# One core, a mixture-of-experts block and a second block: expert biases loaded ahead, the latents' path without GpSimd, late modulation chunks placed anew, the rotary low part in full height

## The chip, the cores and the metric

One Trainium2 chip, one of its cores. The metric is the device time of one execution in microseconds (us), the median of several runs. Besides TensorE (PE), VectorE (DVE), ScalarE (ACT) and GpSimd (POOL) the core has SyncE (SP), which here does nothing but issue loads.

## What is computed

Two transformer blocks on 256 tokens of width 1024, all in 32 bits. The change lies in the first, between its projections and its experts:

```python
m = silu(c) @ w_mod + b_mod                      # 6 chunks of 1024: sh1 sc1 g1 sh2 sc2 g2
hx, hc = modulate(x, g, sh1, sc1), modulate(ctx, g, csh1, csc1)
px, pc = hx @ w_in, hc @ w_in                    # fourier 256, q latent 384, kv latent 256, rope 64
q  = rms_norm(q_lat, norm_q) @ w_q_up            # 6 heads of 128 + 64 rotary
kv = rms_norm(kv_lat, norm_kv) @ w_kv_up         # 6 heads of 128 + 128
att = softmax(q @ k.T * 192**-0.5) @ v           # k from x and from ctx: 512 keys
x  = x + g1 * rms_norm(concat(att, fourier(px)) @ w_out, norm_attn_post)
h  = modulate(x, norm_ffn_pre, sh2, sc2)
logits = h @ w_router + b_router; top 4 of 32 experts for each token
g = min(xb @ w_gate[e] + b_gate[e], 7); u = clip(xb @ w_up[e] + b_up[e], -7, 7)
y = (g * sigmoid(1.702 * g) * (u + 1)) @ w_down[e] + b_down[e]
x  = x + g2 * rms_norm(sum of gates * y, norm_ffn_post)
```

A second block follows (two mixers, two MLPs), which the change does not touch.

## The kernel before, in words

**The stream.** All large weights come in pieces of up to 1 MB through one list of jobs (class `Stream`). Each job has a ring of tiles of its own: ring A (7 tiles), B (6), and C (3), D (2) and E (3), which are opened in SBUF that earlier stages give back. SP issues the loads strictly in the order of the list (line 161); each waits until its tile's earlier content has been read, and a load that waits holds up all behind it. The loads use eight completion semaphores in turn, and a load waits as well until the load that had its semaphore before has landed, whichever engine issued that one. `also` adds small loads behind a job. Ring E is opened by `open_ring` at the start of `moe`, when the tiles of `pre_finish` are free. The expert part of the list is, for each expert, four pieces of `w_gate`, four of `w_up` and four of `w_down`; 21 tiles in all can be ahead.

**Exact products.** Most matmuls before the experts run on pairs: a weight piece is split into a rounded part (ACT) and the rest (a subtraction on DVE, in some cases on POOL: `QA`, `split_aside`), and `mm3` makes three matmuls of them. `prepare` does the splits ahead; ring B holds the pairs.

**The late modulation.** `pre_project` computes sh1 and sc1. The other four chunks of `m` come as 16 pieces of 1 MB, eight for columns 2048 to 4095 (n = 1) and eight for 4096 to 6143 (n = 2). `modulation` takes the next piece: one of n = 1 is four matmuls into the bank `macc` (lines 317 to 319); one of n = 2 is multiplied by `silu(c)` and added into `msum` in four pieces of 512 columns, two of which go to DVE (`scalar_tensor_tensor`, line 311) and two to ACT (line 313) and POOL (line 314). `mod_sum` sums `msum` over the partitions on TensorE, and `mod_fin` turns a result row into columns (ACT copies it to `mrow`, line 329; TensorE transposes it, line 332). The order is all of n = 2, then all of n = 1, and the tables `QMOD`, `MODS` and `FILLS` say how many pieces are taken at which place.

**Latents to attention.** At the end of `pre_project` the latents are scaled by their gains and split, and ACT squares them; POOL adds the squares over the groups of 128 (line 577). `latent_scales` sums them over partitions (`ms`, line 592), takes the root and the reciprocal, and spreads the row over all partitions (diagonals `dgl` on DVE, line 600; `bc`, line 604). It is a generator, called piece by piece from `q_up`, which makes the queries: three weight pairs of 27 matmuls each. `pre_attend` then makes the keys `kn` of six heads, the rotary parts, the values `vt`, and the attention in six steps u (three pairs of heads, two query blocks). A step is `begin(u)` (scores, line 747), `turn(u - 1)` (transposes, line 779), `scores(u)` (the rotary part: `krh` at line 754 with all 128 rows, its low part `krl` at line 755 with the 64 rows of one head; then the softmax on DVE and ACT, lines 759 to 770), and `values` (line 790), with the pieces of `FILLS` at the end. `out_part` is the output projection, whose last matmuls run beside the start of `pre_finish`.

**Into the experts.** `pre_finish` puts small jobs between the parts of the output projection: `bias_rows`, `expert_bias_in` and `bias_split` among them. `expert_bias_in` (line 953) loads the gate and up biases of all experts by four loads on ACT's queue (line 957) and the down biases by four more (line 960); `bias_split` (lines 968 and 971) splits them on ACT and DVE. Only then come, on ACT and DVE, `gained` (lines 888 and 890), `added` (line 899), `turned` (line 905), the norm, the router's logits (line 916), `choose` and the ranks, and the experts' first gather and matmul (lines 1291 and 1208).

## Time and profile before

| what | value |
| --- | --- |
| median of 3 runs | 1835.69 us (1834.64 to 1837.01) |
| the profiled execution's own time | 1836.42 us |
| its span, first to last instruction | 1834.6 us |
| TensorE busy | 1732.3 us, 94% |
| VectorE busy | 752.9 us, 41% |
| ScalarE busy | 589.9 us, 32% |
| GpSimd busy | 57.9 us, 3% |
| bytes moved | 553.45 MB, mean 302 GB/s |

Times in the trace count from the start of the span. A row of the trace names the source line, the engine, the operation, what it writes and reads by the program's names, and how often; several equal instructions in a row are merged into one. What stands in brackets is the idle time of the engine before it and what ended that. TensorE's matmuls on 32 bits appear as two instructions each.

### The profile page before, as it was taken

What the parts mean: (1) busy time and instruction counts of PE and PEld (TensorE: products, weight loads), DVE (VectorE), ACT (ScalarE), POOL (GpSimd) and SP (SyncE); (2) the same over time, 40 slices, a digit from 0 to 9 for tenths busy, and PEclk for the clock granted to TensorE, in tenths of its full rate; (3) what the DMA queues carried; (4) which work ended last, traced back from release to release, by engine and by line L of the source; (5) the groups of instructions that cost most, each with busy time, mean ns of one, the idle gap of its engine ahead of it and who ended that gap; (6) DMA issues with size and microseconds to landing.
All of it is one profiled execution on the core that took longest, in us unless ns stands there. A gap on an engine that the chain in (4) does not pass through costs nothing. (4 is left out here: it accounts for less than half of the span.)

```text
span 1834.6 us, 24464 instructions
## 1 busy us (share of the span) xinstructions
PE 1732.3 (94%) x9537; PEld 1038.8 (57%) x9537; DVE 752.9 (41%) x1582; ACT 589.9 (32%) x1158; POOL 57.9 (3%) x52
## 2 busy tenths in 40 slices
PE   7889599999999989999989988899999999999998
PEld 6756553333333323333323332388689989989997
DVE  4786242222222212222211211476675558756555
ACT  4544221111111101111111110355654445555444
POOL 0340000000000000000000000100000001000000
PEclk9989799999999999999999999999999999999999
DMA  9767599999999999999999999987245554435540
GB/s 350 262 242 265 197 356 405 412 412 411 410 412 413 412 412 412 410 411 412 412 413 412 413 411 411 338 249 230 70 161 186 185 188 154 132 116 203 185 158 23
DMA packets 202525, 553.45 MB, mean 302 GB/s; under 512 B 11136, under 2 KB 87558, under 8 KB 200358
## 3 DMA queue, kind: packets, MB, share of 16 engines
q1 hardware_dynamic: 201026, 549.82, 79.4%
q8 instruction: 76, 1.25, 0.3%
q10 hardware_dynamic: 932, 1.29, 0.2%
q0 software_dynamic: 448, 0.73, 0.1%
q14 instruction: 43, 0.35, 0.1%
HBM read 550.71 MB, written 1.07 MB: 301 GB/s over the span
## 5 line engine op out<-in xcount | busy, mean ns | idle before, releaser
L1565 DVE TENSOR_TENSOR ring<-ring,ring 128x1024 fp32r<-128x1024 f32 x196 | 230.6, 1221 | 78.2 <-ACT ring L1564 77.6
L1208 PE MATMUL g<-ring,xg 128*64 128x512 f32 x1056 | 254.0, 603 | 8.1 <-DMA ring<-in_w_gate 8.1
L1208 PE MATMUL u<-ring,xg 128*64 128x512 f32 x1056 | 248.2, 602 | 10.7 <-DMA ring<-in_w_up 9.7
L1219 PE MATMUL y<-ring,ht 128*64 128x512 f32 x1056 | 241.1, 599 | 15.9 <-DMA ring<-in_w_down 15.4
L1564 ACT CAST ring<-ring 128x1024 fp32r<-128x1024 f32 x196 | 195.3, 1049 | 75.7 <-PE acc L1794 54.3
L1280 ACT ACTIVATE z<-y,gsl 64x512 fp32r<-64x512 f32 x66 | 45.0, 682 | 428.6 <-PE y L1219 401.6
L1779 PE MATMUL ot<-ahi,ring 128*128 128x256 f32 x960 | 177.2, 282 | 0.0
L1219 PEld LDWEIGHTS y<-ring,ht 128*64 128x64 f32 x1056 | 69.9, 136 | 164.6 <-issue 117.6
L1281 DVE SCALAR_TENSOR_TENSOR z<-y,gsl,z 64x512 fp32r<-64x512 f32 x66 | 49.5, 750 | 250.6 <-ACT z L1280 250.5
L1779 PEld LDWEIGHTS ot<-ahi,ring 128*128 128x128 f32 x960 | 151.3, 191 | 1.3
L1208 PEld LDWEIGHTS u<-ring,xg 128*64 128x64 f32 x1056 | 67.3, 136 | 132.5 <-issue 98.9
L1208 PEld LDWEIGHTS g<-ring,xg 128*64 128x64 f32 x1056 | 66.9, 136 | 126.9 <-issue 118.7
L1779 PE MATMUL ot<-alo,ring 128*128 128x256 f32 x480 | 135.6, 283 | 0.0
L1794 PE MATMUL acc<-ring,hhi 128*128 128x512 f32 x480 | 131.5, 395 | 0.0
L1794 PEld LDWEIGHTS acc<-ring,hhi 128*128 128x128 f32 x480 | 88.1, 188 | 19.0
L1227 ACT ACTIVATE sg<-gm 128x512 f32<-128x512 f32 x33 | 20.8, 630 | 238.8 <-DVE gm L1226 238.8
L1779 PEld LDWEIGHTS ot<-alo,ring 128*128 128x128 f32 x480 | 91.8, 191 | 1.3
L1293 ACT ACTIVATE xg<-xg,mod,a 128x128 f32<-128x128 f32 (+1 forms) x136 | 50.9, 452 | 98.3 <-PE xg L1291 98.3
L1779 PE MATMUL pj<-ahi,ring 128*128 128x256 f32 x416 | 80.0, 287 | 0.0
L1291 PEld LDWEIGHTS xg<-pm,x 128*128 128x128 f32 x544 | 63.7, 191 | 26.2 <-issue 14.6
L1270 DVE TENSOR_SCALAR gt<-gt,cp 128x256 fp32r<-128x256 f32 x33 | 16.0, 484 | 150.4 <-PE gt L1268 150.4
L1794 PE MATMUL acc<-ring,hlo 128*128 128x512 f32 x240 | 75.4, 395 | 0.0
(520 smaller groups left out, 2157.2 us busy)
## 6 DMA issues: line engine op xcount, KB each, us to landing
ring<-in_w_gate SPq DMA_DIRECT2D x128, 1024.0 KB, 18.1
ring<-in_w_up SPq DMA_DIRECT2D x128, 1024.0 KB, 18.1
ring<-in_w_down SPq DMA_DIRECT2D x128, 1024.0 KB, 18.1
ring<-in_mlp_w SPq DMA_DIRECT2D x64, 1024.0 KB, 5.3
ring<-in_w_mod SPq DMA_DIRECT2D x24, 1024.0 KB, 7.0
ring<-in_odd_w_in SPq DMA_DIRECT2D x12, 1024.0 KB, 5.7
ring<-in_even_w_in SPq DMA_DIRECT2D x7, 1024.0 KB
ring<-in_w_out SPq DMA_DIRECT2D x4, 1024.0 KB, 5.4
```

The costliest lines, as they stand in the source:

```text
L1208: nc.tensor.matmul(acc[64 * h : 64 * h + 64], xg[:, 2 * q + j], w[:, j, 512 * h : 512 * h + 512], start=(q == 0 and j == 0), stop=False, s ...
L1219: nc.tensor.matmul(acc[64 * h : 64 * h + 64], l, w[:, j, 512 * h : 512 * h + 512], start=(q == 0 and j == 0), stop=(q == 3 and j == 1), sk ...
L1227: nc.scalar.activation(sg, gm, AF.Sigmoid, scale=1.702)
L1270: nc.vector.tensor_scalar(gt, b, self.c("misc")[:, 0:1], None, OP.is_equal)
L1280: nc.scalar.mul(t[s], a[s], g[s])
L1281: nc.vector.scalar_tensor_tensor(t[o], a[s], g[s], t[s].bitcast(F32), OP.mult, OP.subtract)
L1291: nc.tensor.matmul(b[:, n * j : n * j + n], self.x[:, t, (k + j) * P : (k + j + 1) * P], pm[:, t, 0:n], start=(t == 0), stop=(t == 1))
L1293: nc.scalar.activation(xg[:, k + j], b[:, n * j : n * j + n], AF.Identity, bias=self.mod[:, 0, 24 + k + j : 25 + k + j], scale=self.a2[:, ...
L1564: nc.scalar.copy(hi[:, c], v[:, c])
L1565: nc.vector.tensor_tensor(lo[:, c], v[:, c], hi[:, c].bitcast(F32), OP.subtract)
L1779: nc.tensor.matmul(out, w[a][:, k, c : c + n], x[b][:, k], start=(k == 0 and i == 0), stop=(k == KD - 1 and i == 2))
L1794: nc.tensor.matmul(acc[2 * t + n], x[a][kx][:, t * P : (t + 1) * P], w[b][:, j, 512 * n : 512 * n + 512], start=(first and i == 0), stop=( ...
```

## The change

- `expert_bias_in` now only lists the four loads of the gate and up biases, into tiles of their own, and the stream issues them on SP behind the first piece of `w_out`. The four loads of the down biases go to POOL's queue (`down_bias_in`).
- POOL has no arithmetic left before the experts: all subtractions of the splits of `w_q_up` and `w_kv_up` are on DVE, the squares are summed over the groups by TensorE in `latent_scale`, and all four parts of an n = 2 piece are on DVE (the first piece on ACT).
- `latent_scale` is called for the query latent after the first weight pair and for the kv latent after the second, each followed by its `spread`. The split at the end of `pre_project` falls away; the copy of `krp` goes from DVE to ACT.
- The 16 late pieces come in the order `LATE`: one after each weight pair of `q_up`, one after each head's keys, one in each quarter of the values, and one in each of the attention's first three steps. `mod_sum` follows its last piece directly.
- The rotary low part has two tiles of 128 rows, one for each head of a pair, the other head's rows set to zero.

```diff
-MODS, FILLS = (0, 1, 0, 1, 0, 1, 2, 1, 1, 2), (1, 2, 1, 2, 0)
-QMOD, KVA, SMALL, QA, EARLY = 1, 3, 0, 2, 3
+LATE = (1, 1, 1, 2, 1, 2, 1, 2, 1, 2, 2, 2, 2, 1, 1, 2)
+QMODS, MODS, FILLS = (1, 1, 1), (1, 1, 1, 1, 1, 1, 1, 1, 1, 1), (1, 1, 1, 0, 0)
+SMALL, EARLY = 0, 3
...
-                for g in (0, 2, 1, 3):
+                for g in range(4):
                     o, v = self.msum[:, 512 * g : 512 * g + 512], w[:, 512 * g : 512 * g + 512]
                     if k == 0:
                         nc.scalar.mul(o, v, c)
-                    elif g > 1:
+                    else:
                         nc.vector.scalar_tensor_tensor(o, v, c, o, OP.mult, OP.add)
-                    else:
-                        nc.scalar.mul(v, v, c)
-                        nc.gpsimd.tensor_tensor(o, o, v, OP.add)
+                if k == KD - 1:
+                    self.mod_sum()
...
-                (nc.gpsimd if aside else nc.vector).tensor_tensor(l[:, :, i], vv[:, :, i, c0:c1], h[:, :, i].bitcast(F32), OP.subtract)
+                nc.vector.tensor_tensor(l[:, :, i], vv[:, :, i, c0:c1], h[:, :, i].bitcast(F32), OP.subtract)
...
+                ("o", 3): self.expert_bias_in(B)}
...
-        self.late = [(n, k) for n in (2, 1) for k in range(KD)]
+        late = self.late = [(n, LATE[:i].count(n)) for i, n in enumerate(LATE)]
...
-        nc.vector.tensor_copy(krp, br)
+        nc.scalar.copy(krp, br)
-        for s, n in ((sq, 3), (sk, 2)):
-            for j in range(1, n):
-                nc.gpsimd.tensor_tensor(s[:, 0], s[:, 0], s[:, j], OP.add)
-        st.prepare()
...
+    def latent_scale(self, C, i):
+        s, t0, n = self.sq[i], 2 * i, 2 + 2 * i
+        m = s.shape[1]
+        bs = self.bank("ms", "s")
+        for t in range(n):
+            for j in range(m):
+                nc.tensor.matmul(bs[:, 2 * t : 2 * t + 2], s[:, j, t * P : (t + 1) * P], self.c("ones")[:, 0:2], start=(j == 0), stop=(j == m - 1))
+        r = self.r6[:, 2 * t0 : 2 * (t0 + n)]
+        nc.scalar.activation(r, bs[:, 0 : 2 * n], AF.Sqrt, bias=self.eps[1e-6], scale=1.0 / (128 * m))
+        nc.vector.reciprocal(r, r)
+        dg = C.tile([P, 4, P], F32, tag="prob", name="dgl", bufs=3)
+        for t in range(n):
+            nc.vector.tensor_scalar(dg[:, t], self.c("ident"), r[:, 2 * t : 2 * t + 1], None, OP.mult)
+        def spread():
+            b = self.bank("bc", "s")
+            nc.tensor.matmul(b[:, 0 : n * P], self.c("ones"), dg[:, 0:n].rearrange("p a b -> p (a b)"), start=True, stop=True)
+            nc.scalar.copy(self.rqk[:, t0 * P : (t0 + n) * P], b[:, 0 : n * P])
+        return spread
...
-            next(scales, None)
+            if q < 2:
+                spread = self.latent_scale(C, q)
...
-            if q == QMOD:
-                self.modulation()
+            self.modulation(QMODS[q])
+            if q < 2:
+                spread()
...
+        kr[2] = B.tile([P, 512], F32R, tag="krp", name="krl1")
+        zero = self.c("tri")[:, 0:1].to_broadcast([P, 512])
+        nc.scalar.copy(kr[2][0:64], zero[0:64])
+        nc.scalar.copy(kr[2][64:P], kr[1][64:P].bitcast(F32))
+        nc.vector.tensor_copy(kr[1][64:P], zero[64:P])
...
-                nc.tensor.matmul(b, l[o], kr[1][o], start=False, stop=True)
+                nc.tensor.matmul(b, l, kr[1 + i], start=False, stop=True)
...
-        fills = {u: [self.mod_sum] * (u == 2) + [self.modulation] * FILLS[u] + [gains] * (u == 4) for u in range(5)}
+        fills = {u: [self.modulation] * FILLS[u] + [gains] * (u == 4) for u in range(5)}
...
-        fills = [lambda: self.bcast_row(C, self.gc, g1b, bank="b"), router, lambda: self.bias_rows(B), lambda: self.expert_bias_in(B, R),
+        fills = [lambda: self.bcast_row(C, self.gc, g1b, bank="b"), router, lambda: self.bias_rows(B), lambda: self.down_bias_in(R),
...
-            t = self.braw[nm] = B.tile([P, 512], F32, tag=tag, name="braw")
+            t = self.braw[nm] = B.tile([P, 512], F32, name=f"{nm}r")
             for h in range(2):
-                self.nc.scalar.dma_start(out=t[64 * h : 64 * h + 64], in_=bass.AP(tensor=b.tensor, offset=b.offset + 512 * h, ap=[[0, 2], [D, E], [1, 512]]))
+                loads.append((t[64 * h : 64 * h + 64], bass.AP(tensor=b.tensor, offset=b.offset + 512 * h, ap=[[0, 2], [D, E], [1, 512]])))
...
-            self.nc.scalar.dma_start(out=self.bdn[E * q : E * q + E], in_=self.I["b_down"][0][:, T * q : T * q + T])
+            self.nc.gpsimd.dma_start(out=self.bdn[E * q : E * q + E], in_=self.I["b_down"][0][:, T * q : T * q + T])
```

Three places show how the order of instructions moves. The first is ACT's queue at the end of the output projection (`braw` are the raw biases, `bdn` those of the down matrices, `bkt` a small row for the second block). Before:

```order
L262 COPY gu<-bc 128x512 x2
L1695 ACTIVATE bkt<-bk 16x384
L957 DMA braw<-in_b_gate 64x1x512 x2
L957 DMA braw<-in_b_up 64x1x512 x2
L960 DMA bdn<-in_b_down 32x256 x4
L968 CAST b_gate<-braw 128x512
L968 CAST b_up<-braw 128x512
L888 ACTIVATE jk,s_1678<-mix 128x512 x2
```

and of the change:

```order
L265 COPY gu<-bc 128x512 x2
L1696 ACTIVATE bkt<-bk 16x384
L969 CAST b_gate<-b_gater 128x512
L969 CAST b_up<-b_upr 128x512
L885 ACTIVATE jk,s_1673<-mix 128x512 x2
```

The loads have left this queue, and the two casts read the tiles that the stream loads. The four loads now stand in SP's queue, behind the first of the four `w_out` pieces:

```order
L164 DMA ring_1036<-in_w_mod 128x2048
L164 DMA ring_1066<-in_w_out 128x2x1024
L164 DMA b_gater<-in_b_gate 64x1x512 x2
L164 DMA b_upr<-in_b_up 64x1x512 x2
L164 DMA ring_1092<-in_w_out 128x2x1024
L164 DMA ring_1114<-in_w_out 128x2x1024
```

Three `w_out` pieces and all the experts' pieces are queued behind them. The third place is DVE from the rotary keys to the attention's first softmax. Before:

```order
L718 TENSOR_TENSOR krl<-krp,krh 128x512
L311 SCALAR_TENSOR_TENSOR msum<-ring_825,csil,msum 128x512 x2
L311 SCALAR_TENSOR_TENSOR msum<-ring_827,csil,msum 128x512 x2
L311 SCALAR_TENSOR_TENSOR msum<-ring_829,csil,msum 128x512 x2
L311 SCALAR_TENSOR_TENSOR msum<-ring_831,csil,msum 128x512 x2
L1677 COPY vc_1119<-bk 128x64
```

and of the change:

```order
L711 TENSOR_TENSOR krl_1039<-krp,krh 128x512
L716 CAST krl_1039<-cp 64x512
L314 SCALAR_TENSOR_TENSOR msum<-ring_886,csil,msum 128x512 x4
L314 SCALAR_TENSOR_TENSOR msum<-ring_930,csil,msum 128x512 x4
L314 SCALAR_TENSOR_TENSOR msum<-ring_944,csil,msum 128x512 x4
L314 SCALAR_TENSOR_TENSOR msum<-ring_976,csil,msum 128x512 x4
L1678 COPY vc_1138<-bk 128x64
```

DVE has 16 accumulations here where it had 8; the 8 additions that POOL made beside them are gone.

## Rows read from the trace of the kernel before

**Rows 1.** Busy by stretch (start:end us; length, busy us per engine, granted clock, DMA share, GB/s).
```profile
1000.00:1100.00 100.00, 90.30 (x418) 32.89 (x418) 18.75 (x38) 13.32 (x28) 0.00 (x0) 1.00 1.03 411
```

**Rows 2.** Queue of SP, who waited for whom: us in total, times, longest us.
```profile
SPq L161 <- DMA braw<-in_b_gate: 17.6, 1, 17.6
...
SPq L161 <- DMA braw<-in_b_up: 15.3, 2, 7.9
```

**Rows 3.** SyncE's queue in order of time around 229 us (start us, us, what).
```profile
229.00 0.88 SPq L161 DMA_DIRECT2D ring<-in_w_down  x2
```

**Rows 4.** ScalarE in order of time, 191 to 214 us (in brackets: idle before, releaser).
```profile
191.26 1.24 ACTq L957 DMA_DIRECT2D braw<-in_b_gate  x2
...
213.46 0.62 ACT L968 CAST b_up<-braw 128x512 fp32r<-128x512 f32 x1 [12.58 <-DMA braw<-in_b_up]
```

**Rows 5.** TensorE in order of time, 191 to 238 us.
```profile
191.09 8.46 PE L361 MATMUL mix<-ring,mix 128*128 128x512 f32 x36
...
218.32 1.94 PE L905 MATMUL bk<-cp,x 128*128 128x128 f32 x8 [18.77 <-DVE x L899]
...
220.08 3.62 PE L916 MATMUL lb<-wr,x1T 128*128 128x32 f32 x16
...
236.14 1.94 PE L1208 MATMUL g<-ring,xg 128*64 128x512 f32 x8
```

**Rows 6.** VectorE in order of time, its last operation on the biases.
```profile
214.11 1.38 DVE L971 TENSOR_TENSOR b_up<-braw,b_up 32x512 fp32r<-32x512 f32 x2 [11.81 <-ACT b_up L968]
```

**Rows 7.** Busy by stretch as in rows 1, the stretch of the routing.
```profile
215.00:229.00 14.00, 10.68 (x50) 10.26 (x50) 7.89 (x21) 8.38 (x20) 0.00 (x0) 0.50 0.55 222
```

**Rows 8.** TensorE in order of time: four forms at full clock.
```profile
120.50 1.07 PE L319 MATMUL macc<-ring,csil 128*32 128x512 f32 x8
...
139.34 0.48 PE L754 MATMUL sc<-krh,qs 128*128 128x512 f32 x1
...
139.74 0.49 PE L755 MATMUL sc<-krl,qs 64*128 64x512 f32 x1
...
157.41 1.04 PE L779 MATMUL tr<-cp,prob 128*128 128x128 f32 x8
```

**Rows 9.** TensorE in order of time, the query projection, 70 to 78 us.
```profile
70.03 0.50 PE L592 MATMUL ms<-cp,sqk 128*128 128x2 f32 x4
...
77.08 1.19 PE L604 MATMUL bc<-dgl,cp 128*128 128x256 f32 x2 [3.21 <-DVE dgl L600]
```

**Rows 10.** VectorE by line and form, 60 to 125 us: count, busy us, mean ns.
```profile
L311 DVE SCALAR_TENSOR_TENSOR msum<-ring,csil,msum 128x512 f32<-128x512 f32 x14 | 21.7, 1605 | 0.0
...
L566 DVE SCALAR_TENSOR_TENSOR lk<-bk,vc,lk 128x512 fp32r<-128x512 f32 x2 | 1.4, 748 | 1.6 <-ACT lk L565 1.6
```

**Rows 11.** VectorE in order of time, first step of the attention.
```profile
124.98 1.27 DVE L759 TENSOR_REDUCE mx<-sc 128x1 f32<-128x512 f32 x2
```

**Rows 12.** TensorE in order of time, steps of the attention.
```profile
127.90 1.97 PE L779 MATMUL tr<-cp,prob 128*128 128x128 f32 x8 [2.33 <-DVE prob L770]
...
155.69 1.88 PE L747 MATMUL sc<-kn,qn 128*128 128x512 f32 x4
...
161.73 1.88 PE L747 MATMUL sc<-kn,qn 128*128 128x512 f32 x4
```

**Rows 13.** DMA queues from 190 to 216 us: packets, MB, share of 16 engines.
```profile
q10 hardware_dynamic: 456, 0.66, 8.2%
```

**Rows 14.** ScalarE in order of time, the second split of the output projection.
```profile
162.38 2.01 ACT L1564 CAST ring<-ring 128x1024 fp32r<-128x1024 f32 x2
```

**Rows 15.** Busy by stretch as in rows 1, four stretches before the experts.
```profile
120.00:146.00 26.00, 21.14 (x86) 9.12 (x85) 15.66 (x35) 7.69 (x18) 3.72 (x3) 0.80 0.81 311
...
146.00:166.00 20.00, 19.24 (x89) 10.83 (x85) 12.54 (x29) 8.10 (x17) 0.00 (x0) 1.00 0.60 211
...
166.00:196.00 30.00, 29.77 (x138) 23.48 (x139) 11.70 (x27) 9.93 (x17) 0.56 (x1) 1.00 0.74 287
...
196.00:229.00 33.00, 14.23 (x66) 12.88 (x64) 10.14 (x24) 10.54 (x24) 0.00 (x0) 0.60 0.59 207
```

More of the change, by code (lines that the diff above doesn't have):

```diff
@@ L614, in q_up @@
         held = []
[L615 to L616 removed]
+        self.r6 = C.tile([P, 12], F32, name="r6")
+        self.rqk = B.tile([P, 768], F32, name="rqk")
         for q in range(3):
@@ L629, in q_up @@
                 held = []
-            if q == 1:
-                next(scales)
             st.prepare()
-            if q == QMOD:
-                self.modulation()
+            self.modulation(QMODS[q])
+            if q < 2:
+                spread()
+        self.msum = B.tile([P, 2048], F32, tag="sqk", name="msum")
     def pre_attend(self, B, C):
```

48 lines of the change are left out of this document (12 added, 36 removed).

## The prediction

> **What bounds the kernel now.** I read the page first, then busy time by stretch, then the waits of SP's queue, and last the time lines of the engines from 60 to 240 us. The long middle, the experts, is bound by loading: late in it the DMA engines are full at 411 GB/s, while TensorE has work for 90 of 100 us [rows 1]. The experts' last weight therefore lands a fixed time after the moment from which the loads run without a break. That moment is when ring E opens and the last three of the 21 tiles can be filled, at 229.00 us [rows 3], 7 us before the experts' first matmul at 236.14 [rows 5]. What comes after the experts waits for them. So the change is worth what it moves this moment, and I follow the path to it.
>
> Two places on that path are to be seen. The large one: TensorE ends the output projection at 191.09 + 8.46 = 199.55 us and then waits 18.77 us for `added` on DVE [rows 5]. ACT issued the bias loads at 191.26, and its cast of the up biases ran only at 213.46, after an idle time put down to that load [rows 4]; DVE's subtraction follows at 214.11 [rows 6], and everything of `pre_finish` is queued behind these on both engines. The same loads held up SP's queue for 17.6 and 15.3 us [rows 2]. The granted clock of the stretch behind the idle time is 0.50, the lower of the two levels, 1.2 GHz [rows 7]. The second: the attention's first reduction runs at 124.98 [rows 11], behind DVE's accumulations of the late modulation, which took 1605 ns in the mean, where the same operation at the same size takes 748 when POOL does nothing [rows 10].
>
> **The change, part by part.** *The bias wait.* From the end of DVE's last bias operation, 214.11 + 1.38 = 215.49, to the transposes at 218.32 [rows 5, 6] the path needs 2.83 us. It starts from the second bank of the projection. The last part makes 24 of the 36 matmuls of that row, bank by bank, so the second bank is done at 191.09 + 8.46 × 24/36 = 196.7. With the biases there, the casts and subtractions can run from 191.3 on and need 0.62 + 2 × 1.38 = 3.4 us, which ends at 194.7, beside the projection. The transposes could start at 196.7 + 2.83 = 199.6, where TensorE is free at 199.55. Of 18.77 us I take **18.6** away. Ends: 18.8, and 12 if `gained` has to wait for something that the biases hid.
>
> *The clock behind it.* From 218.32 to 236.14 TensorE does two blocks of transposes (1.94 each) and two of logits (3.62 each) [rows 5] at half clock. Transposes of that form take 1.04 at full clock [rows 8]; by the same ratio the logits take 1.9 (an estimate). Without the idle time there is no reason for the low clock, and 0.9 + 0.9 + 1.7 + 1.7 = 5.2 us less are on TensorE. The second transposes wait for `added(1)` and ACT's copies all the same, so I take the two logits: **3.4**. Ends: 0 (the short idle times of the routing are enough to lower it again) and 5.2.
>
> *POOL's work to DVE.* Before the attention DVE does 24 accumulations where it did 14. At 14 × 1605 ns they were 21.7 us busy; 24 at 0.7 (two take 1.4 [rows 10]) are 16.8. The first reduction comes **4.9** earlier, near 120.1. The second tile of the rotary low part costs DVE a copy of half height and ACT two, beside a subtraction that POOL no longer slows; I set these against each other. Ends: 0, and 5.8, where the scores themselves would be late next. The score matmuls cost nothing: 0.48 us with 128 rows, 0.49 with 64 [rows 8].
>
> *The query projection.* The sums over partitions take 16 more instructions at 0.50/4 us [rows 9], 2.0 us, and three pieces of the modulation at 1.07 [rows 8] come in, 3.2. Against this stand the wait of 3.21 for the diagonals [rows 9], which are now made before the next pair's splits, and the two pieces (2.1) that stood between values and attention. I count **0**, ends 3 less and 4 more. The splits' subtractions that come to DVE there fill time in which it waited for the row scales. The three pieces among the heads lie beside DVE, which sets the pace there.
>
> *The attention's steps.* From the first reduction to the fifth `begin` (161.73) it takes 36.75 us now [rows 11, 12]. Anew, at full clock: 2.9 to the first transposes (124.98 to 127.90); transposes and scores 2.5; the n = 1 row must pass ACT's two exponentials and its copy, 3.6; `begin`, transposes and scores 4.2 (a full cycle is 161.73 − 155.69 = 6.04, of which `values` is about 1.8, estimates from these rows). In the third step `mod_sum` now waits on TensorE's queue until DVE has done the softmax (2.9), the `mix` subtraction (0.4) and four accumulations (2.8), and then for ACT's copy and the transposes: 7.6, with all later steps queued behind it; then two cycles of 6.04. The sum is 32.9, or 3.9 less. But TensorE stands still for some 4 us there, and after the 2.33 us before the first transposes its clock was low now (those took 1.97 where full clock gives 1.04 [rows 8, 12]). I leave **1.0** of it, ends 3.9 less and 3 more.
>
> *The bias loads on SP.* They are issued near 114 us; the second `w_out` piece, which stood behind no such loads, is next and would land near 119 (5.4 us on the page). Its split starts at 162.38 [rows 14], now near 156.5, so 37 us of delay are covered. ACT's queue with these loads used 8.2% of 16 engines in 26 us [rows 13], 34 us of one engine, four fifths of it for the four loads: 27 us on one engine, 1.7 spread over 16. Either way it costs nothing. The Trainium skill, "DMA: Bandwidth & Descriptors", the section on why a DMA increments its semaphore by 16, says that such a load is divided over the largest number of engines up to 16 that divides the slowest dimension of both sides, and always uses the lowest-numbered ones. These loads have 2 there, so by that rule all four would sit on the same two engines and push two sixteenths of every later piece back by about 13.5 us; the sum stays, and the slower rival below gets 0.04 where I would have given it 0.01. No run here shows which engines served a load.
>
> *Room for the loads.* From 120 to 229 us the DMA engines stood idle for 26 × 0.20 + 20 × 0.40 + 30 × 0.26 + 33 × 0.41 = 34.5 us [rows 15], more than the gain. The down biases on POOL's queue are used far into the experts and cost nothing.
>
> **Sum.** 18.6 + 3.4 + 4.9 + 0 + 1.0 = 27.9 us. The profiled execution took 1836.42, so 1808.5; its span of 1834.6 becomes 1806.7. The median of the runs, 1835.69, lies 0.7 below the profiled one and gives 1807.8. I forecast **1808 us**, by itself 1800 to 1816.
>
> **Rivals.** *The clock stays low.* If the stop in the third step and the short waits of the routing bring half clock, the second term is 0 and the last is 3 more: 18.6 + 4.9 − 3 = 20.5 less, **1816**. For it: the idle times of 18.77 and 2.33 us were each followed by it [rows 5, 7, 8, 12]. Against: the output projection in between ran long and dense.
>
> *DVE becomes the bound.* If the accumulations stay at 1.6 us without POOL, 24 of them take 38.5 where 21.7 stood, 16.8 more before the attention, and four more cost 3.6 in the third step: 18.6 + 3.4 − 16.8 − 2.6 = 2.6 less, **1834**. Against it: the 748 ns.
>
> *The loads don't follow.* If the tiles can't be filled sooner, because each waits for the stage that frees it, ring E opens on time but the stream is no further: **1836**. The 34.5 us speak against it.
>
> *Slower.* The four bias loads run one after another at the head of SP's queue, each as slow as all four together now (191.26 to 213.46, 22.2 us): 88.8 us, and the second `w_out` piece lands at 119 + 89 = 208 in place of 156.5. That is 51 late, less 27.9: **1859**. It decides from a delay of 37 + 28 = 65 us on. For it: four loads of 128 KB needed 22.2 us in a queue of their own. Against it: the 27 us of one engine.
>
> **Chances.** Forecast 0.70, low clock 0.20, DVE 0.03, loads 0.03, slower 0.04. The range 1800 to 1822 holds the first two with the bounds of their terms. Within 0.2% (3.7 us, about what a measurement of this kernel can tell from no change) lie DVE and loads, 0.06.
>
> **What would show it.** Right: no wait of TensorE over 1 us between the output projection and the transposes; logits near 1.9 us; ring E's first load near 201 and the experts' first matmul near 208; the first reduction near 120; accumulations near 0.7 us; `mod_sum` some 6 us behind the third step's scores. Wrong: a new wait before the output projection for `w_out`, or a DMA share under 0.95 in the experts' first 100 us, or an experts' start that moved and an end that did not.

## The result and the profile after

The changed kernel takes **1806.26 us** (median of 4 runs, 1803.48 to 1808.73) where the kernel before, beside it, takes 1835.16 (1832.76 to 1837.01): a ratio of 0.9843, 95% interval 0.9824 to 0.9862. The forecast was 1808 in a range of 1800 to 1822. The profiled execution has a span of 1803.7 us, 31.0 less than before. The head of its page:

```profile
span 1803.7 us, 24461 instructions
## 1 busy us (share of the span) xinstructions
PE 1721.6 (95%) x9553; PEld 1031.0 (57%) x9553; DVE 744.8 (41%) x1604; ACT 583.3 (32%) x1147; POOL 22.8 (1%) x31
```

TensorE, the end of the output projection and what follows, in order of time:

```profile
178.97 8.46 PE L363 MATMUL mix<-ring,mix 128*128 128x512 f32 x36
187.69 1.29 PE L902 MATMUL bk<-cp,x 128*128 128x128 f32 x8 [0.26 <-DVE x L896]
188.99 1.97 PE L913 MATMUL lb<-wr,x1T 128*128 128x32 f32 x16
...
197.28 0.41 PE L1009 MATMUL ranks<-mask,cp 128*128 128x32 f32 x2 [1.34 <-DVE mask L1002]
```

and ScalarE's two casts of the biases in the same stretch:

```profile
179.47 0.60 ACT L969 CAST b_gate<-b_gater 128x512 fp32r<-128x512 f32 x1
179.98 0.62 ACT L969 CAST b_up<-b_upr 128x512 fp32r<-128x512 f32 x1
```

The idle time of 18.77 us [rows 5] is 0.26 us; the casts, which waited for their loads [rows 4], run while the projection goes on; a block of logits takes 1.97 us where it took 3.62. The experts' first matmul comes at 203.50 us (236.14 before).

VectorE, the 16 accumulations ahead of the attention and the first reduction in order of time, and then the group of all accumulations (busy, mean ns of one):

```profile
105.53 10.69 DVE L314 SCALAR_TENSOR_TENSOR msum<-ring,csil,msum 128x512 f32<-128x512 f32 x16
...
116.93 1.28 DVE L756 TENSOR_REDUCE mx<-sc 128x1 f32<-128x512 f32 x2
```

```profile
L314 DVE SCALAR_TENSOR_TENSOR msum<-ring,csil,msum 128x512 f32<-128x512 f32 x28 | 18.9, 747 | 0.1
```

They follow each other 0.67 us apart, and the first reduction answers to [rows 11]: 116.93 in place of 124.98. TensorE in the attention's steps:

```profile
119.86 1.78 PE L776 MATMUL tr<-cp,prob 128*128 128x128 f32 x8 [2.33 <-DVE prob L767]
...
126.15 0.66 PE L334 MATMUL bk<-cp,mrow 128*128 128x128 f32 x4 [1.70 <-ACT mrow L331]
...
134.68 3.03 PE L321 MATMUL macc<-msum,cp 128*32 128x512 f32 x8 [2.62 <-DVE msum L314]
...
138.45 0.66 PE L334 MATMUL bk<-cp,mrow 128*128 128x128 f32 x4 [0.73 <-ACT mrow L331]
138.94 1.88 PE L745 MATMUL sc<-kn,qn 128*128 128x512 f32 x4
...
144.19 1.88 PE L745 MATMUL sc<-kn,qn 128*128 128x512 f32 x4
```

Here is the new stop: `mod_sum` waits 2.62 us for VectorE, then takes 3.03 where 1.07 is its own work, and its transposes wait 0.73 more. But a full cycle, from one `begin` to the next, is 5.25 us (138.94 to 144.19), where it was 6.04 [rows 12].

Last, busy time by stretch (columns as in [rows 1]). The changed kernel in the 2 us ahead of ring E's opening, at the experts' start, in 2 us of it by themselves, and late in the experts; then the kernel before in the 2 us ahead of its own opening:

```profile
193.75:195.75 2.00, 2.00 (x15) 1.84 (x14) 1.19 (x5) 1.92 (x5) 0.93 (x1) 1.00 0.15 59
198.00:206.00 8.00, 7.51 (x33) 5.26 (x32) 4.60 (x31) 2.16 (x8) 0.87 (x1) 0.57 0.97 377
206.00:208.00 2.00, 2.00 (x14) 1.28 (x14) 0.27 (x1) 0.48 (x2) 0.00 (x0) 1.00 0.28 20
1000.00:1100.00 100.00, 89.77 (x400) 30.29 (x398) 17.87 (x34) 11.82 (x24) 0.00 (x0) 1.00 1.03 412
```

```profile
227.00:229.00 2.00, 2.00 (x11) 2.00 (x11) 0.00 (x0) 1.92 (x5) 0.00 (x0) 0.50 0.00 0
```

The late experts are as full of transfers as before (1.03). In both kernels the DMA engines have nearly run dry when ring E opens (shares of 0.15 and 0.00). From 198 to 206 the granted clock is 0.57 in the mean, so the lower level (1.2 GHz) held for most of it: it came back, behind the 1.34 us that `ranks` waits for `mask`, and at the very place where the experts begin. From 206 to 208 the loads pause once more (0.28, 20 GB/s).

The budget of the two profiled executions, from the starts and ends of these rows and of those before (the sixth `begin` of the kernel before is the row at 161.73 [rows 12], which the prediction calls the fifth):

| stretch | before | after | difference | forecast |
| --- | --- | --- | --- | --- |
| start to query projection | 66.70 | 63.70 | -3.00 | 0 |
| query projection to first reduction | 58.28 | 53.23 | -5.05 | -4.9 |
| first reduction to the sixth `begin` | 36.75 | 32.51 | -4.24 | -1.0 |
| that to the end of the output projection | 37.82 | 37.99 | +0.17 | 0 |
| idle time | 18.77 | 0.26 | -18.51 | -18.6 |
| transposes to the opening of ring E | 10.68 | 8.06 | -2.62 | -3.4 |
| opening to the load behind the experts' first finished tile | 9.12 | 10.69 | +1.57 | 0 |
| that load to the end of the span | 1596.51 | 1597.24 | +0.73 | 0 |
| sum | 1834.63 | 1803.68 | -30.95 | -27.9 |

The load in the last two rows is the second `w_gate` load after the opening; it can be issued only when the experts' first four matmul pairs have given back their tile. SyncE's queue in order of time, before and after:

```profile
238.12 0.37 SPq L161 DMA_DIRECT2D ring<-in_w_gate  x1
```

```profile
195.75 0.37 SPq L164 DMA_DIRECT2D ring<-in_w_down  x1
...
206.44 0.37 SPq L164 DMA_DIRECT2D ring<-in_w_gate  x1
```

### The profile page after: what moved, and what is told of

It reads as the page before. It is cut to its first block, busy times and chain, and to the rows that moved or that the text cites. A ratio compares the mean times of both kernels' runs of the same rounds, so it can differ in the third digit from the quotient of the medians.

```text
span 1803.7 us, 24461 instructions
## 1 busy us (share of the span) xinstructions
PE 1721.6 (95%) x9553; PEld 1031.0 (57%) x9553; DVE 744.8 (41%) x1604; ACT 583.3 (32%) x1147; POOL 22.8 (1%) x31
## 3 DMA queue, kind: packets, MB, share of 16 engines
HBM read 550.71 MB, written 1.07 MB: 306 GB/s over the span
## 4 chain that ended last, share of the span: by engine, by line
PE 72%; DMA 18%; DVE 6%; ACT 3%; issue 1%; SPq 0%; ACTq 0%; DVEq 0%
PE acc L1795 11%; PE g L1209 10%; PE u L1209 10%; PE ot L1780 10%; PE y L1220 8%; DMA ring<-in_w_gate 7%; DMA ring<-in_w_up 5%; DMA ring<-in_w_down 4%; PE pj L1780 4%; PE xg L1292 3%; PE pj L1787 2%; PE yb L1362 1%; PE bk L542 1%; PE mix L363 1%; DVE msum L314 1%
## 5 line engine op out<-in xcount | busy, mean ns | idle before, releaser
L1566 DVE TENSOR_TENSOR ring<-ring,ring 128x1024 fp32r<-128x1024 f32 (+1 forms) x200 | 234.3, 1215 | 77.8 <-ACT ring L1565 77.3
L1565 ACT CAST ring<-ring 128x1024 fp32r<-128x1024 f32 (+1 forms) x200 | 198.5, 1046 | 75.7 <-PE acc L1795 54.3
```

Of the source, the lines that this page charges most:

```text
L1565: nc.scalar.copy(hi[:, c], v[:, c])
L1566: nc.vector.tensor_tensor(lo[:, c], v[:, c], hi[:, c].bitcast(F32), OP.subtract)
```

## The experiments

My theory after the result: the terms of the sum add, and of the larger gain up to ring E's opening (33.25 us against 27.9) a part is lost behind it. Its rivals: that the parts overlap, and that the loads before the opening bind. This table puts all kernels side by side (us; the first four columns from the profiled execution).

| kernel | ring E opens | load behind the first finished tile | between them | that load to the end | median of runs | ratio to before, 95% interval |
| --- | --- | --- | --- | --- | --- | --- |
| before | 229.00 | 238.12 | 9.12 | 1596.5 | 1835.2 | |
| the change | 195.75 | 206.44 | 10.69 | 1597.2 | 1806.3 | 0.9824 to 0.9862 |
| e1_bias_alone | 208.00 | 215.32 | 7.32 | 1596.9 | 1813.5 | 0.9869 to 0.9902 |
| e2_all_but_bias | 221.07 | 230.83 | 9.76 | 1597.1 | 1828.8 | 0.9958 to 0.9983 |
| e3_half_height | 200.05 | 207.35 | 7.30 | 1596.2 | 1806.3 | 0.9840 to 0.9874 |
| e4_modsum_later | 201.00 | 208.30 | 7.30 | 1596.7 | 1807.1 | 0.9841 to 0.9873 |
| e5_change_again | 196.41 | 207.22 | 10.81 | 1597.1 | 1807.4 | 0.9837 to 0.9867 |
| e6_row_late | 193.82 | 201.13 | 7.31 | 1596.5 | 1799.3 | 0.9786 to 0.9813 |
| e7_row_late_low_aside | 189.75 | 197.06 | 7.31 | 1597.5 | 1796.3 | 0.9769 to 0.9796 |
| e8_bias_spread | 196.95 | 207.42 | 10.47 | 1597.2 | 1807.3 | 0.9832 to 0.9863 |
| e9_gpsimd_busy | 201.78 | 212.61 | 10.83 | 1598.8 | 1811.8 | 0.9855 to 0.9885 |
| e10_aside_half | 189.08 | 199.56 | 10.48 | 1598.0 | 1799.4 | 0.9800 to 0.9826 |
| e11_aside_again | 192.44 | 200.15 | 7.71 | 1597.5 | 1797.1 | 0.9780 to 0.9806 |
| e12_gpsimd_beside | 203.44 | 214.20 | 10.76 | 1598.4 | 1815.5 | 0.9877 to 0.9915 |

**e1_bias_alone.** The kernel before, with the biases moved alone:

```diff
-                ("q", 2): [...], ("k", SMALL): self.post_small()}
+                ("q", 2): [...], ("k", SMALL): self.post_small(),
+                ("o", 3): self.expert_bias_in(B)}
...
-            lambda: self.expert_bias_in(B, R),
+            lambda: self.down_bias_in(R),
```

> The kernel before with the bias loads moved alone (gate and up biases behind the first w_out piece on SyncE's queue, down biases on GpSimd's queue); everything else as before. Theory A (the bias wait is the large term and nothing stands behind it): TensorE's idle time of 18.8 us before the transposes falls under 1 us, transposes and logits run at full clock, ring E opens near 229.0 - 18.5 - 2.6 = 207.9 us, and the kernel takes about 20 us less than before (1815). Theory B (the parts overlap: alone, gained has to wait for something that the biases hid): idle time of some 7 us stays and the gain is about 12 us (1823).

Measured: 20.3 us less than the kernel before beside it (1833.8). TensorE in order of time:

```profile
191.22 8.46 PE L361 MATMUL mix<-ring,mix 128*128 128x512 f32 x36
199.93 1.29 PE L906 MATMUL bk<-cp,x 128*128 128x128 f32 x8 [0.26 <-DVE x L900]
201.24 1.97 PE L917 MATMUL lb<-wr,x1T 128*128 128x32 f32 x16
```

Theory A: 0.26 us idle, ring E at 208.00 (207.9 was written), and a gain of 20.3 us where about 20 were. No wait of any size stands behind the bias wait.

**e2_all_but_bias.** The changed kernel with `expert_bias_in` as before, on ScalarE's queue (the diff of e1 reversed).

> The changed kernel with the bias loads back in their old place on ScalarE's queue. Theory A (the terms add): the idle time of 18 to 19 us before the transposes and the low clock behind it return; ring E opens about 21 us later than in the changed kernel (217), and of the gain 9 to 12 us are left (1824 to 1827). Theory B (the loads of the experts bind first, so that what is moved before the projection is not seen at the end): at most 4 us of gain are left (1831 to 1835).

Measured: 5.0 us less than before. TensorE behind the projection:

```profile
210.39 1.94 PE L901 MATMUL bk<-cp,x 128*128 128x128 f32 x8 [19.18 <-DVE x L895]
212.15 3.62 PE L912 MATMUL lb<-wr,x1T 128*128 128x32 f32 x16
```

The wait and the low clock are back, as theory A says; but ring E opens 25.3 us later than in the change, and not 21, and the 5.0 us that are left lie between the two theories. In this profile the attention from the first reduction to the sixth `begin` takes 35.17 us, 2.66 more than in the change, in stretches of low clock, and the query projection starts 1.18 later. These 3.84 us are most of what is missing from theory A. The two parts make 20.3 + 5.0 = 25.3 against 28.9 together. Each of the three 95% intervals reaches 2 to 4 us to either side, so the runs agree with terms that add and don't show it to better than that. Against theory B the DMA engines say more than the 5.0 us: here, too, they stood idle (share 0.00) in the 2 us ahead of ring E's opening.

**e3_half_height.** The changed kernel without the second low tile:

```diff
-        kr[2] = B.tile([P, 512], F32R, tag="krp", name="krl1")
...
-                nc.tensor.matmul(b, l, kr[1 + i], start=False, stop=True)
+                nc.tensor.matmul(b, l[o], kr[1][o], start=False, stop=True)
```

> The changed kernel with the rotary low part in half height again (64 rows, one tile). Theory A (the forecast: height costs nothing): the four rotary matmuls of a step take the same time on TensorE in both heights, the attention's cycle stays 5.25 us, and the time is within 1 us of the changed kernel (1806). Theory B (a matmul of 64 rows holds up the matmuls next to it): the four take 1.9 us instead of 1.5, the cycle is 5.7 us, ring E opens 2 to 3 us later and the kernel takes 2 to 3 us more (1808 to 1809).

Measured: the same time, and yet theory B in the steps. `begin` in order of time on TensorE:

```profile
141.83 1.88 PE L740 MATMUL sc<-kn,qn 128*128 128x512 f32 x4
...
147.87 1.88 PE L740 MATMUL sc<-kn,qn 128*128 128x512 f32 x4
```

The cycle is 6.04 us, 0.79 more than with full height. The weight loads (PEld) of the four rotary matmuls show where, first of the change, then of e3_half_height:

```profile
146.78 0.19 PEld L752 LDWEIGHTS sc<-krl,qs 128*128 128x128 f32 x1
147.02 0.19 PEld L751 LDWEIGHTS sc<-krh,qs 128*128 128x128 f32 x1
147.25 0.19 PEld L752 LDWEIGHTS sc<-krl,qs 128*128 128x128 f32 x1
```

```profile
150.78 0.18 PEld L748 LDWEIGHTS sc<-krl,qs 64*128 64x128 f32 x1 [0.24 <-issue]
151.21 0.19 PEld L747 LDWEIGHTS sc<-krh,qs 128*128 128x128 f32 x1 [0.24 <-issue]
151.63 0.18 PEld L748 LDWEIGHTS sc<-krl,qs 64*128 64x128 f32 x1 [0.24 <-issue]
```

Of one height, the loads follow each other 0.23 us apart, beside the matmuls. Of two heights they are 0.43 apart, of which the weight load takes 0.19 and stands still for 0.24, as if load and matmul took turns. The time did not move because ring E opened 4.3 us later but the load behind the first finished tile came only 0.9 later: here the clock stayed full at the experts' start (granted 1.00, where the change had 0.57), and the loads do not pause:

```profile
202.00:210.00 8.00, 7.88 (x50) 4.77 (x49) 4.87 (x33) 2.97 (x10) 0.90 (x1) 1.00 1.02 400
```

The Trainium skill, "TensorEngine Tiling (Array Packing)", section "Key Properties", says that a change of the tiling mode, and not just of the tile, drains TensorE. The 0.43 us agree with it; the rows show only the standstill, not that a drain is its cause.

The 4.3 us are not the price of the height alone. Without the three copies of the second low tile the first reduction comes 33.00 us after the keys' rotary matmul, in the change 34.83: 1.83 sooner. The steps from there to the sixth `begin` take 5.60 us more, of which the two cycles are 1.56 and much of the rest is low clock (granted 0.53 from 126.05 to 131.00, where the same work of the change, from 126.64 to 131.00, had 1.00).

**e4_modsum_later.** The changed kernel with `mod_sum` in the fourth step:

```diff
-                if k == KD - 1:
-                    self.mod_sum()
...
-        fills = {u: [self.modulation] * FILLS[u] + [gains] * (u == 4) for u in range(5)}
+        fills = {u: [self.modulation] * FILLS[u] + [self.mod_sum] * (u == 3) + [gains] * (u == 4) for u in range(5)}
```

> The changed kernel with mod_sum one step later (in the fourth step, a step after its last piece). TensorE's stop in the third step (2.6 us idle, then a mod_sum of 3.0 us where 1.07 is its own work, then 0.7 idle) should go, and ring E open 4 to 5 us earlier than in the changed kernel (191 to 192). Theory A (the end is a fixed time after ring E opens): the kernel takes 4 to 5 us less (1801 to 1802). Theory B (at the opening the loads issued before it have not landed yet: the DMA engines were 0.87 busy in the 20 us before it, so only 2.6 us can be won there): the opening moves by 4 to 5 us and the end by less than 2.6 (1804 to 1806).

Measured: no gain, and ring E later, not earlier. TensorE:

```profile
141.11 1.06 PE L319 MATMUL macc<-msum,cp 128*32 128x512 f32 x8
146.99 1.11 PE L332 MATMUL bk<-cp,mrow 128*128 128x128 f32 x4 [4.82 <-ACT mrow L329]
```

`mod_sum` itself no longer waits (1.06 us), but its transposes wait 4.82 us for `mrow`: ScalarE's copy stands behind the two exponentials of the step and ran at 146.33. One wait took the place of the other. Of the 5.25 us by which ring E opens later, 3.81 were lost ahead of the first reduction (120.74 against 116.93), where the edit changes nothing, and the full clock at the experts' start gave 3.4 back. Both theories rested on an edit that did not do what it said, so it tells them apart no further.

**e5_change_again.** No edit.

> The changed kernel once more, beside the next three. In the six profiles so far the low clock did not fall in the same stretches. Theory A (it follows from the idle times, which the program sets): again low clock from about 119.8 to 123.2 and from 198.3 to 205.1 us and nowhere else before the experts, span within 1 us of 1803.7. Theory B (behind equal idle times it comes or not): at least one of the stretches is absent or a new one of 3.4 us or more is there, as in the kernel before at 21.5 us behind the same idle time of 2.11 us, and the start of the query projection or of the experts moves by 1 to 3 us with it. In both, the span ends 1596.2 to 1597.3 us after the load that waits for the experts' first finished tile is issued (206.44 in the first profile), as in all six profiles.

Measured: 1807.44 against 1835.25 before. Theory B: the low clock at the experts' start came again, and a new stretch of it came at the beginning. The stretch from 21 to 29 us, behind the same idle time of 2.11 us in each, in the kernel before, the change, and the change again (granted clock is the third number from the right):

```profile
21.00:29.00 8.00, 6.73 (x24) 5.78 (x24) 5.26 (x10) 3.60 (x7) 0.00 (x0) 0.57 1.07 367
```

```profile
21.00:29.00 8.00, 6.47 (x60) 4.87 (x61) 5.52 (x11) 4.26 (x9) 0.00 (x0) 1.00 1.07 366
```

```profile
21.00:29.00 8.00, 7.27 (x56) 5.67 (x56) 4.79 (x9) 3.05 (x6) 0.00 (x0) 0.79 1.07 366
```

The query projection starts at 63.70 in the first profile of the change and at 64.41 in the second; over the eleven profiles that have the change's code up to there it lies between 63.70 and 67.26, with 64.68 in the middle, so the first profile is the earliest of all. And the load behind the first finished tile is again 1597.1 us before the end.

**e6_row_late.** The changed kernel with the last n = 2 piece a step earlier, and `mrow` copied a step ahead of the transposes:

```diff
-LATE = (1, 1, 1, 2, 1, 2, 1, 2, 1, 2, 2, 2, 2, 1, 1, 2)
+LATE = (1, 1, 1, 2, 1, 2, 1, 2, 1, 2, 2, 2, 2, 1, 2, 1)
...
-                    self.mod_fin(self.macc, n)
+                    nc.scalar.copy(self.mrow, self.macc)
...
+        fills[2].insert(0, self.mod_sum)
+        fills[3] = [lambda: self.mod_fin(1), lambda: nc.scalar.copy(self.mrow, self.sacc)]
+        fills[4] = [lambda: self.mod_fin(2), gains]
```

> The changed kernel with the last n = 2 piece in the second step in place of the third, mod_sum in the third, and the copies to mrow one step ahead of the transposes that read them, so that TensorE waits for neither DVE nor ACT there. TensorE's stops of 1.70, of 2.62 with a stuttering mod_sum (3.03 where 1.07 is its own) and of 0.73 us should go: 7.0 us, of which the softmax of the second and third step takes 1 to 2 back. Theory A (the end is a fixed time after the load behind the experts' first finished tile): that load is issued 5 to 6 us earlier (201) and the span is 1798 to 1799. Theory B (the loads before the opening bind now): the load is issued earlier and the end moves by less than 2 us (1802 or more).

Measured: 1799.34, 8.1 us under the change beside it. TensorE:

```profile
133.37 1.07 PE L319 MATMUL macc<-msum,cp 128*32 128x512 f32 x8
...
140.59 0.60 PE L330 MATMUL bk<-cp,mrow 128*128 128x128 f32 x4
...
142.94 1.12 PE L741 MATMUL sc<-kn,qn 128*128 128x512 f32 x2 [0.88 <-ACT prob L759]
```

The stops are gone; from the first reduction to the sixth `begin` it takes 27.40 us in place of 32.51. Theory A: the load at 201.13, the span 1797.6, and 1596.5 us between them. Against the profile of e5 (the two spans lie 6.7 us apart) the steps give 5.1 and the full clock at the experts' start 3.5 (7.31 us there in place of 10.81); 3.0 were lost ahead of the first reduction, where the edit changes nothing. That the load came at the time that was written is therefore in part the clock's doing.

**e7_row_late_low_aside.** As e6, with the low part made between the accumulations:

```diff
             self.modulation(MODS[6 + t])
+            if t == 1:
+                nc.scalar.copy(kr[0], krp)
+                nc.vector.tensor_tensor(kr[1], krp, kr[0].bitcast(F32), OP.subtract)
+        kr[2] = B.tile([P, 512], F32R, tag="krp", name="krl1")
...
```

> As e6_row_late, with the rotary low part made later: the rounding and its subtraction behind the second quarter of the values, the zero halves behind the fourth, so that DVE's 16 accumulations do not start behind ScalarE's three copies. Theory A (DVE sets the first reduction): the accumulations start 2 to 3 us earlier, the first reduction comes 1.5 to 2.5 us earlier than in e6_row_late and the end with it. Theory B (TensorE's own work, the values, sets it): the first reduction moves by less than 0.5 us.

Measured: 1796.31, 3.0 under e6. VectorE:

```profile
104.75 5.38 DVE L314 SCALAR_TENSOR_TENSOR msum<-ring,csil,msum 128x512 f32<-128x512 f32 x8
...
110.65 5.38 DVE L314 SCALAR_TENSOR_TENSOR msum<-ring,csil,msum 128x512 f32<-128x512 f32 x8
...
117.45 1.28 DVE L753 TENSOR_REDUCE mx<-sc 128x1 f32<-128x512 f32 x2
```

Counted from the rotary matmul of the keys the first reduction comes after 32.93 us, in e6 after 34.82: 1.89 less, theory A. From 104.15 to the first reduction VectorE has no idle time in the trace; it sets this stretch.

**e8_bias_spread.** The changed kernel with each load of the gate and up biases cut in two, so that its slowest size is 32:

```diff
-                loads.append((t[64 * h : 64 * h + 64], bass.AP(..., ap=[[0, 2], [D, E], [1, 512]])))
+                for r in range(2):
+                    loads.append((t[64 * h + E * r : 64 * h + E * r + E], bass.AP(..., ap=[[D, E], [1, 512]])))
```

> The changed kernel with the gate and up biases in eight loads of 32 rows in place of four of 2 times 32. Theory A (the forecast: by the rule of the Trainium skill, DMA: Bandwidth & Descriptors, four loads whose slowest size is 2 sit on two engines and hold up two sixteenths of every later piece): the first w_gate piece lands within 7 us of its issue in place of 19.4, the issues of the next four loads take 0.4 us each in place of 1.2 to 2.5, and the time does not change (1805 to 1807), since 37 us of delay are covered. Theory B (the delay of the first gate pieces counts): the time falls by 2 us or more.

Measured: no difference in time (1807.27 against 1807.44). What moved, from the view of DMA between 104 and 144 us (median us to landing; GB/s in slices of 1 us), first of the change, then of e8_bias_spread:

```profile
GB/s 369 344 98 66 33 37 332 410 295 51 45 90 199 297 272 328 289 272 274 279 281 297 270 356 406 430 401 393 188 66 49 53 53 90 233 438 360 41 45 147
...
ring<-in_w_gate SPq DMA_DIRECT2D x4, 1024.0 KB, 19.4
```

```profile
GB/s 352 328 295 115 90 25 78 381 426 352 254 64 47 295 438 401 406 442 397 446 397 401 410 299 401 426 70 8 0 0 0 0 0 0 41 336 410 262 0 0
...
ring<-in_w_gate SPq DMA_DIRECT2D x4, 1024.0 KB, 12.3
```

Behind the four loads the queue moves some 280 GB/s for 10 us and a gate piece lands after 19.4 us; behind the eight, some 400 and 12.3. The "within 7 us" was wrong: three `w_out` pieces stand ahead of it. The rule of the Trainium skill ("DMA: Bandwidth & Descriptors", the section on why a DMA increments its semaphore by 16) agrees in direction; the delay is 7.1 us, where the estimate of 13.5 was worked out from it, and no run shows which engines served a load. Theory A on the time: a delay of this size is covered.

**e9_gpsimd_busy** and **e12_gpsimd_beside.** The changed kernel with work for GpSimd behind each n = 2 piece; in e9 all four additions read `cp`, in e12:

```diff
+                if k:
+                    for g in range(4):
+                        nc.gpsimd.tensor_tensor(self.idle, self.cp[:, 0:256], self.cp[:, 256:512] if g else self.msum[:, 1536:1792], OP.add)
```

> The changed kernel with four additions of 256 columns on GpSimd beside each n = 2 piece from the second on; they read constants and write a tile that nobody reads, so nothing waits for them. Theory A (it is GpSimd's work that slows the accumulations on VectorE, as the term of the forecast assumes): accumulations that run beside it take over 1.0 us in place of 0.68, the first reduction comes 3 us or more later than in the changed kernel (117 to 118), and the span ends 2 us or more later. Theory B (they were slow before for another reason, such as the ScalarE passes over the same tile): they stay at 0.68 to 0.75 us and nothing moves.

Measured: 1811.84, but the question was missed: nothing held the additions, and they ran from 4.6 to 31.2 us, beside no accumulation. The accumulations stay at 747 ns. Beside the additions VectorE's `xh` (line 442, two of 128x1024) took 1.89 us in place of 1.42; what of the 4 to 5 us comes from there and what from the clock stays open.

> As e9_gpsimd_busy, whose additions ran from 4.6 to 30.4 us and so beside no accumulation: now the first of each four reads the last part of msum, so that they start behind a piece and run beside the accumulations of the next. Theory A (GpSimd's work slows the accumulations on VectorE): those that run beside it start more than 1.0 us apart in place of 0.68; the 16 accumulations before the attention take 14 us or more in place of 10.7, the first reduction comes 2 to 5 us later against the start of the attention's keys, and ring E opens later with it. Theory B (they were slow in the kernel before because of ScalarE's passes or the wait for GpSimd's result): they stay 0.68 us apart and the 16 take 10.7 us.

Measured: 1815.51, and theory A. VectorE and then GpSimd in order of time:

```profile
107.30 15.89 DVE L314 SCALAR_TENSOR_TENSOR msum<-ring,csil,msum 128x512 f32<-128x512 f32 x16
...
123.91 1.27 DVE L760 TENSOR_REDUCE mx<-sc 128x1 f32<-128x512 f32 x2
```

```profile
111.38 3.33 POOL L317 TENSOR_TENSOR idle<-cp 128x256 f32<-128x256 f32 x3
```

The same 16 accumulations take 15.89 us in place of 10.69 with GpSimd at work beside them, on other data, and the first reduction comes 5.96 us later counted from the keys, more than the 2 to 5 that were written. The first four ran before GpSimd's additions started at 110.19. The other twelve, and after them the last eight ahead of the attention in the kernel before (ns of the shortest, the middle and the longest; first and last start):

```profile
L314 DVE SCALAR_TENSOR_TENSOR msum<-ring,csil,msum x12: 743/1210/1225, 110.0 to 122.0; 128x512 f32<-128x512 f32 x12
```

```profile
L311 DVE SCALAR_TENSOR_TENSOR msum<-ring,csil,msum x8: 1745/1754/1776, 110.7 to 122.5; 128x512 f32<-128x512 f32 x8
```

Beside the additions they start 1.09 us apart in place of 0.67, as was written. In the kernel before it was 1.69. e12 does not reach that: its additions have 256 columns and other data, those of the kernel before had 512 and wrote into `msum`, behind ScalarE's passes. In both, one accumulation goes with about one addition of GpSimd (a start every 1.14 us in e12, every 1.66 in the kernel before). So it is shown that GpSimd's work slows VectorE; that it was the whole cause in the kernel before is not.

**e10_aside_half** and **e11_aside_again.** e7 with half height (the diff of e3), and e7 once more.

> As e7_row_late_low_aside with the rotary low part in half height (one tile, 64 rows, without the three copies). Theory A (a matmul of 64 rows between others of 128 keeps the next weight load from running beside the matmul ahead of it, as the cycle of 6.02 us in e3_half_height against 5.25 says): the four rotary matmuls of a step take 1.7 us in place of 1.0, steps that TensorE bounds take 0.7 us more, and ring E opens and the kernel ends 2 to 4 us later than e7_row_late_low_aside (1798 to 1800). Theory B (the copies that fall away on DVE and ScalarE pay for it): within 1 us of it.

> e7_row_late_low_aside once more, beside e10_aside_half: 1795 to 1797, and span minus issue of the load behind the experts' first finished tile again 1596.2 to 1597.5 us.

Measured: 1799.41 and 1797.11. Half height reaches the first reduction 0.70 us sooner (32.23 against 32.93, the copies), needs 1.42 more from there to the sixth `begin` (27.81 against 26.39) and 0.77 more in the sixth step, gets 0.5 back in the projection, and is 1.0 later at its end (97.90 against 96.88 from the keys' rotary matmul). So full height is worth 1.0 us in that arrangement, between the two theories; in the first steps the softmax on VectorE covers part of it, which is a reading and was not tested. The rest of the 2.3 us between the medians is not settled: e10's profile has the low clock at the experts' start, e11's has not.

## Why the prediction was right, and where it was not

**The path** was right, its last link was not. "The experts' last weight lands a fixed time after the moment when ring E opens" fails: opening and end lie 1605.6 us apart before and 1607.9 after. Over all 14 profiles that distance goes from 1603.5 to 1609.6. Loads still under way are not the reason: in both kernels the DMA engines were nearly idle in the 2 us ahead of the opening (0.00 and 0.15). What differs lies behind it. At the low clock TensorE gave back the experts' first tile later, and until the next load could follow the loads paused (0.28 and 20 GB/s from 206 to 208); in e3, at full clock, they did not. Of the signs that were named, the opening (195.75) and the experts' first matmul (203.50) are some 5 us earlier than written, the first reduction (116.93) 3 us, and the DMA share of the experts' first 100 us is 0.98. What is fixed is the time behind the load that waits for the experts' first finished tile: 1596.2 to 1598.8 us in all 14 profiles, while that load moves from 238.12 to 197.06. In e3 the opening comes 4.30 us later than in the change, that load 0.91, and the span is 0.1 shorter: the opening alone hastens nothing. That this very load sets the end, and not another event beside it at the experts' start, is not shown.

**Bias wait**, -18.6: measured -18.51, and shown alone by e1. The 2.83 us from the last bias operation and the second bank at 196.7 were the right reading (e1's transposes start at 199.93, 199.6 was written): casts and subtractions lie beside the projection, and TensorE waits 0.26 us.

**The clock behind it**, -3.4: -2.62 up to the opening. The logits take 1.97 us (1.9 was written) and the transposes 1.29. Behind the opening the lower level came back and took 1.57. The rival "the clock stays low" was therefore half true, at another place: in six of the twelve kernels without the bias wait (the change, e5, e8, e9, e10, e12) the stretch from the opening to the load takes 10.5 to 10.8 us, in the others 7.3 to 7.7. What decides it stays open.

**GpSimd's work to VectorE**, -4.9, and **query projection**, 0: -5.05 together: 4.09 from the keys' rotary matmul to the first reduction (38.92 to 34.83) and 0.96 ahead of it. The 748 ns of [rows 10] held (747). e12 shows that GpSimd's work slows the accumulations on VectorE (1.09 us apart in place of 0.67), but not that it made all of the 1.69 of the kernel before. The 4.09 have the copies of the next paragraph in them; without these it would be some 5.9 (an estimate from 4.09 and 1.83), just past the far end of 5.8.

**Rotary low part**, 0: this step failed in both its halves, and that its net came out small is luck. The prediction compared the busy time of single rows, 0.48 and 0.49 us [rows 8]. The rows overlap; what counts is the distance from one start to the next, and both rows of [rows 8] came from a group with a half-height matmul in it. A cycle of one height is 0.79 us shorter. The copies of the second tile, which were set against a faster subtraction, are not free either: they hold up the first reduction by 1.83 us (e3), and e7, which moves them, wins 1.89.

**The attention's steps**, -1.0 left of 3.9 worked out: -4.24. The worked-out sum of 32.9 us was nearly met (32.51), by errors that cancel. The stop of `mod_sum` is there, as described: from the third step's scores, which end at 130.34, to the next `begin` at 138.94 it is 8.6 us, of which `values` take 1.9; 7.6 were written. `mod_sum` starts 4.3 us behind the scores where 6 were written, since it takes `msum` part by part while VectorE still makes the next, and lasts 3.03. The two cycles behind it take 10.50 in place of 12.08, by the term above. What was wrong is the 2.9 taken off the sum for the low clock: it held for only 3.4 us, and the transposes and scores of that stretch took 3.42 us (119.86 to 123.28) where 2.5 were written.

**Start to query projection**, not in the sum: -3.00. 2.42 of it lie in the projections, where the clock was 0.57 in one profile and 1.00 in the other behind the same idle time; it belongs to the two executions, not to the change (e5 starts the query projection 0.71 later than the change with no edit). 0.58 is the shorter wait for `sqk`.

**Bias loads on SP**, 0, and **room for the loads**: both held. No wait for `w_out` appears, a delay of the gate pieces of 7 us is covered (e8), and the loads followed an opening as early as 189.08 (e10). The rivals that rest on the accumulations, on loads that don't follow and on bias loads that hold up `w_out` fell with that.

So 27.9 us came true as 28.9 in the medians (27.8 in e5) by terms that were right to 1 us where they were large; that the sum is so close is partly luck. In the two profiled executions, 30.95 us apart, 3.0 at the start and 3.2 in the steps came on top of the forecast, and 3.3 were lost elsewhere, 1.57 of it behind the opening; the medians lie 2 us closer together than these two executions.

## What to carry to other kernels

Where a queue feeds a long stretch that is bound by transfers, look for the event behind which the end stands at a fixed distance by comparing several kernels, not by its name: here the first tile given back kept that distance, and the ring that opened did not. Price a matmul by the distance between starts, with its neighbours, and look at the weight loads' row when heights differ. Where an engine waits in order for a copy on another engine, try issuing the copy a step ahead: moving the sum alone (e4) only changed what it waited for, while moving sum and copy (e6) shortened the steps by 5.1 us. With the low part moved as well (e7, e11) the kernel takes 1796 to 1797 us, the best version here.

## What the runs showed that was not expected

The lower clock came or did not come behind the same idle time: behind 2.11 us at the start the granted clock of the next 8 us was 1.00 and 0.79 in two profiles of the changed kernel, and 0.57 in the kernel before. Behind 1.34 us at the experts' start it came in six kernels of twelve. There the two pairs of equal programs agree (low in the change and e5, full in e7 and e11), so it may hang on the program; a second wait of some 0.5 us follows in five kernels (the change, e5, e9, e11, e12), four of which are among the six, and e8 and e10 fell without it. The lower clock is worth 3.4 us at the experts' start and up to 2.4 at the beginning, together about as much as the spread of the runs of one kernel (1803.48 to 1808.73). A single profile therefore does not price a term of this size.

GpSimd slowed VectorE's two-input operations although they shared no data: from 0.67 to 1.09 us an accumulation in e12. It slowed operations with one tensor input too: from 1.42 to 1.89 us for two normalizations in e9.
